# The activations' pool closed after the attention and opened again 64 bytes on

## The chip, the cores and the metric

The kernel runs on one core of a Trainium2 chip. The metric is the device time of one launch in microseconds (us). TensorE (PE) does matmuls, VectorE (DVE) and ScalarE (ACT) element-wise work, GpSimd (POOL) a little of it and DMA descriptors; SyncE (SP) only issues DMAs.

## The reference

Two layers over `x` of 512 tokens by 1024, all in fp32. The first is dilated attention, the second an mLSTM mixer; each is followed by a SwiGLU feed-forward block.

```python
def reference(x, ...):
    h = x
    h = h + dilated_attention_mixer(rms_norm(h, attn_norm[0]), positions, attn_w_in[0], attn_w_out[0])
    h = h + swiglu(rms_norm(h, ffn_norm[0]), ffn_w_in[0], ffn_w_out[0])
    h = h + mlstm_mixer(rms_norm(h, mlstm_norm[0]), mlstm_w_in[0], ..., mlstm_w_out[0])
    h = h + swiglu(rms_norm(h, ffn_norm[1]), ffn_w_in[1], ffn_w_out[1])
    return rms_norm(h, final_norm)

def swiglu(xn, w_in, w_out):           # D_FF = 2816
    gu = xn @ w_in
    return (jax.nn.silu(gu[..., :D_FF]) * gu[..., D_FF:]) @ w_out
```

## The kernel before, in words

**Arithmetic.** Each fp32 operand of a matmul is split in two fp32r parts, a high half (a copy on ACT, names in `_h`) and a low half (value minus high, on DVE, names in `_l`). A product is three matmuls: high by high, low by high, high by low (`SPLITS`). `h` is kept as eight tiles `h0` to `h7` of 128 features by 512 tokens. Normed activations `n1` (for the first feed-forward block) are split likewise into `n1_h0` to `n1_h3` and `n1_l0` to `n1_l3`, each holding two of the eight tiles; the norm's factor is applied after the product.

**Stages around the change.** The attention ends with the output projection: `awo0` to `awo3`, each 256 output features in two banks, from the split heads `ao_h0` to `ao_h3`, `ao_l0` to `ao_l3`. Its last part `awo3` runs through `project` (line 280): two chunks of four tiles, and for each chunk both banks. DVE adds each bank to `h` (line 1431), ACT squares `h` (`n1sq`, line 420), DVE sums the squares (`n1ssum`, line 421). Then `norm("ffn", 0, "n1", ssum)` (line 1981) takes eight tiles with `x_tiles` and splits `h` into them (lines 262 and 263), and `ffn_in` begins with `plain(0)`: the four banks `f0j0_00`, `f0j0_01`, `f0j0_10`, `f0j0_11` from `n1` and the split weights of `f0j0`, whose tiles have the same names with `_w`, `_h`, `_l` (in those the second digit is the chunk, and the first is gate or up). In the middle stands the sum over tokens for the norm (`n1ss`, then a Newton iteration from `n1v` to `n1dg` on DVE, then `n1bc` on PE).

**Order.** The scheduler of the framework sets the order of each engine's instructions: it takes what is ready by its own reckoning of releases, where the code doesn't tie instructions together (`fenced`, `run`, `issue_after`). Engines run their instructions strictly in that order and wait on semaphores.

**Places.** A pool takes its memory at the end of the one before it, and inside a pool a tag has a place, in the order in which tags are first used. The order of pools is `const`, `act`, `gap0` (64 bytes), `w`, `gap1` (448 bytes), `h`, `norm`, and after them the pools of the running stage (attention, `ffn0`, `mlstm`, `ffn1`). `act` has eight tags `x0` to `x7` of 4 KB a partition. They hold in turn `xa` and `ao` (attention), `n1`, the hidden tiles 3 to 10 of the first feed-forward block, `n2`, `yo`, `n3`, and hidden tiles again. The first user of the pool is `idle_w` with tag `x7` (line 108), so that `x7` lies at the pool's start and `x0` to `x6` behind it. A tile waits for the last reader of what lay in its place: `n1_h0` (tag `x0`) lies where `ao_h0` lay, and so on, pair by pair.

Of the kernel before, what the change touches and what calls it, by code (L numbers as in the profile page):

```python
# [11 lines left out]
F32 = mybir.dt.float32  # L12
# [5 lines left out]
P = 128  # L18
# [57 lines left out]
def tile_hybrid_dilated_attn_mlstm(  # L76
# [8 lines left out]
    def pool(stack, name, **kw):  # L85
        return stack.enter_context(tc.tile_pool(name=name, bufs=1, **kw))

    cp = pool(ctx, "const")
    xp = pool(ctx, "act")
    gap0 = pool(ctx, "gap0")  # L90
    wp = pool(ctx, "w")
    gap1 = pool(ctx, "gap1")
    ps = pool(ctx, "psum", space=bass.MemoryType.PSUM)


# [43 lines left out]
    def col(key, i):  # L139
        return cols[:, row_of[key] + i:row_of[key] + i + 1]  # L140
# [7 lines left out]
    def defer(n, fn):  # L148
        later.append((tick[0] + n, next(order), fn))
# [106 lines left out]
    def split_act(hi, lo, src, gain):  # L256

        if gain is None:
            nc.scalar.activation(hi, src, AF.Copy)
            nc.vector.tensor_tensor(lo, src, hi.bitcast(F32), op=ALU.subtract)  # L260
        else:
            nc.scalar.activation(hi, src, AF.Copy, scale=gain)
            nc.vector.scalar_tensor_tensor(lo, src, gain, hi.bitcast(F32), op0=ALU.mult, op1=ALU.subtract)

    def x_tiles(name):
        parts = [xp.tile([P, 2, SEQ], F32R, tag="x%d" % i, name="%s_%s%d" % (name, "hl"[i % 2], i // 2))
                 for i in range(KC)]
        return [[parts[k // 2 * 2 + part][:, k % 2] for k in range(KC)] for part in range(2)]
# [104 lines left out]
    def inverse_rms(v, name, box=None, then=None):  # L373

        r = npl.tile([P, TB], F32, tag="rtok", name=name + "r", bufs=2)
        rbc = npl.tile([P, SEQ], F32, tag="rbc", name=name + "rbc")
        parts = {}

        def finish():
            nc.vector.tensor_scalar(v, v, 1.0 / D, EPS, op0=ALU.mult, op1=ALU.add)  # L380
            rsqrt_newton(npl, v, TB, name + "r", r)
            rhl = npl.tile([P, 2, TB], F32R, tag="rhl", name=name + "rhl", bufs=2)
            nc.vector.tensor_copy(rhl[:, 0], r)
            nc.vector.tensor_tensor(rhl[:, 1], r, rhl[:, 0].bitcast(F32), op=ALU.subtract)
            for part in range(2):
                dg = parts[part] = npl.tile([P, SEQ], F32R, tag=("ssum", "sq")[part], name=name + "dg",
                                               bufs=1 + part)
                for tb in range(TB):
                    nc.vector.tensor_scalar(dg[:, tb * P:(tb + 1) * P], ident,
                                            rhl[:, part, tb:tb + 1].bitcast(F32), None, op0=ALU.mult)  # L390

        def hook():
            bp = ps.tile([P, 512], F32, tag="t", name=name + "bc", bufs=1)
            for part in range(2):
                nc.tensor.matmul(bp, ones_r, parts[part], start=(part == 0), stop=(part == 1))
            nc.vector.tensor_copy(rbc, bp)
            if then is not None:
                then(bp)
        if box is None:
            finish()  # L400
        else:
            box["finish"] = finish
        return rbc, r, hook


    w_in = attn_w_in[0]
    hp = pool(ctx, "h")
    npl = pool(ctx, "norm")
    h = [hp.tile([P, SEQ], F32, tag="h", name="h%d" % k, bufs=KC + 1) for k in range(KC)]

    def squares_of(name):

        ssum = npl.tile([P, SEQ], F32, tag="ssum", name=name + "ssum")

        def add(k):
            if k == 0:
                nc.scalar.activation(ssum, h[k], AF.Square)
            else:
                sq = npl.tile([P, SEQ], F32, tag="sq", name=name + "sq", bufs=2)
                nc.scalar.activation(sq, h[k], AF.Square)  # L420
                nc.vector.tensor_tensor(ssum, ssum, sq, op=ALU.add)
        return ssum, add
# [1057 lines left out]
    def norm(key, k0, name, ssum=None, wait=1):  # L1480
        pair = x_tiles(name)
        add = None
        if ssum is None:
            ssum, add = squares_of(name)
        for k in range(KC):
            split_act(pair[0][k], pair[1][k], h[k], col(key, k0 + k))
            if add is not None:
                add(k)
        v = npl.tile([P, TB], F32, tag="rs_v4", name=name + "v", bufs=2)
        box = {}  # L1490

        def sums():
            sp = ps.tile([P, 512], F32, tag="t", name=name + "ss", bufs=1)
            for tb in range(TB):
                nc.tensor.matmul(sp[:, tb:tb + 1], ssum[:, tb * P:(tb + 1) * P], ones[:, 0:1],
                                 start=True, stop=True)
            nc.vector.tensor_copy(v, sp[:, :TB])
            box["finish"]()
        rbc, r, hook = inverse_rms(v, name, box)
        defer(wait, sums)  # L1500
        return pair, rbc, r, hook
# [253 lines left out]
    def output_products(layer, fp, wo, sums_of_rows):  # L1755
# [222 lines left out]
            return [(kind, ops[(a, b) if kind == "product" else b], whl[a, b]) for kind, a, b in items[-TAIL:]]  # L1978
        return hid, during, prepare, work

    pair, rbc, _, hook = norm("ffn", 0, "n1", ssum)
    with ExitStack() as fctx:
        fp = pool(fctx, "ffn0")
# [25 lines left out]
        old, h = h, []  # L2009
# [565 lines left out]
```

## Time and profile before

| what | value |
|---|---|
| median of 3 runs | 1357.41 us (1357.39 to 1357.9) |
| the profiled execution's own time | 1358.57 us |
| its span | 1356.8 us |
| TensorE busy | 1340.1 us, 99% |
| VectorE busy | 1133.0 us, 84% |
| ScalarE busy | 813.3 us, 60% |
| GpSimd busy | 196.7 us, 14% |

The profile is of one execution. A row of a timeline has start and length in us, engine, line, operation, `out<-in` with buffer numbers left out (`n_h` is any of `n1_h0`, ...), shape and count, and in brackets the idle time before it with what ended it. A matmul's length is longer than the step to the next one, since matmuls are pipelined; the steps are read from starts, or from the chain of work that ended last, which has start, length and count of a run of matmuls.

### The profile page before, as it was taken

The numbers are of one execution on the slowest core, as the hardware profiler recorded it, in microseconds if no ns is written. First come the engines' busy times: TensorE is split into PE (matmuls) and PEld (weight loads), VectorE is DVE, ScalarE is ACT, GpSimd is POOL, SyncE is SP. The second block draws the span as 40 slices with busy tenths as digits, with TensorE's granted clock in tenths as the row PEclk, the third lists the DMA queues.
The fourth block names the chain that finished last, engine by engine and source line by source line (L and its number), as shares of the span: only waits on it lengthen the run. The fifth ranks groups of instructions, "written<-read, shape, count | busy, mean of one in ns | idle before, by whom it ended". The sixth has DMA issues, their size and how long they took to land.

```text
span 1356.8 us, 23343 instructions
## 1 busy us (share of the span) xinstructions
PE 1340.1 (99%) x9100; PEld 1222.1 (90%) x9100; DVE 1133.0 (84%) x1787; ACT 813.3 (60%) x1303; POOL 196.7 (14%) x272
## 2 busy tenths in 40 slices
PE   9999999999999999999999999999999999999997
PEld 7898899999988888999999998898878899999886
DVE  7988789899876389888888898898848988997887
ACT  6676577667674255555577464795534555558854
POOL 3000013141412001000010110122200112112113
PEclk9999999999999999999999999999999999999999
DMA  9354244554676357343362743324333545447863
GB/s 306 122 181 155 79 141 143 169 172 155 184 261 191 125 142 172 114 125 125 125 156 79 171 126 87 100 63 124 94 118 97 127 133 172 141 136 173 189 171 101
DMA packets 141270, 194.90 MB, mean 144 GB/s; under 512 B 9028, under 2 KB 106116, under 8 KB 141160
## 3 DMA queue, kind: packets, MB, share of 16 engines
q1 hardware_dynamic: 120128, 140.73, 33.0%
q0 software_dynamic: 19808, 52.48, 16.1%
q8 instruction: 71, 1.16, 0.3%
q10 hardware_dynamic: 1224, 0.21, 0.1%
q14 instruction: 39, 0.32, 0.1%
HBM read 167.30 MB, written 22.54 MB: 140 GB/s over the span
## 4 chain that ended last, share of the span: by engine, by line
PE 79%; DVE 10%; ACT 3%; issue 3%; DMA 1%; POOL 0%; SPq 0%; ACTq 0%; DVEq 0%; POOLq 0%
PE fo L1996 7%; PE f1j_u L1681 5%; PE f0j_u L1681 5%; PE f1j_c L1681 4%; PE f0j_c L1681 4%; PE f1j_p L1681 4%; PE f0j_p L1681 4%; PE mwo L275 3%; PE f1j L275 3%; PE f0j L275 3%; PE mqk L275 3%; PE awo L275 3%; PE finp L2411 3%; PE mo L275 3%; PE finc L2411 2%
## 5 line engine op out<-in xcount | busy, mean ns | idle before, releaser
L1803 POOL DMA_DIRECT2D f0S<-in_ffn_w_out_dram x10 | 8.7, 874 | 248.9 <-DVE f0hid L1720 162.3
L2364 POOL DMA_DIRECT2D hD<-hB x32 | 20.7, 655 | 109.6 <-DVE hB L2361 109.4
L1828 POOL DMA_DIRECT2D f1T<-in_ffn_w_out_dram x15 | 17.8, 1186 | 86.1 <-ACT f1T L1831 40.8
L240 DVE TENSOR_TENSOR v1P_l<-v1W,v1P_h 128x1024 fp32r<-128x1024 f32 x14 | 17.1, 1224 | 10.3 <-ACT v1P_h L238 10.3
L275 PE MATMUL mo<-n_h,mo_k_h 128*128 128x512 f32 x64 | 25.7, 401 | 0.0
L275 PE MATMUL mwo<-yo_h,mwo_k_h 128*128 128x512 f32 x64 | 25.5, 398 | 0.0
L275 PE MATMUL awo<-ao_h,awo_k_h 128*128 128x512 f32 x64 | 25.5, 398 | 0.0
L275 PE MATMUL mwo<-yo_l,mwo_k_h 128*128 128x512 f32 x64 | 25.5, 398 | 0.0
L275 PE MATMUL mwo<-yo_h,mwo_k_l 128*128 128x512 f32 x64 | 25.5, 398 | 0.0
L275 PE MATMUL mo<-n_h,mo_k_l 128*128 128x512 f32 x64 | 25.4, 397 | 0.0
L275 PE MATMUL mqk<-n_h,mqk_k_h 128*128 128x512 f32 x64 | 25.4, 397 | 0.0
L275 PE MATMUL mo<-n_l,mo_k_h 128*128 128x512 f32 x64 | 25.4, 396 | 0.0
L275 PE MATMUL mqk<-n_l,mqk_k_h 128*128 128x512 f32 x64 | 25.3, 396 | 0.0
L275 PE MATMUL awo<-ao_l,awo_k_h 128*128 128x512 f32 x64 | 25.3, 396 | 0.0
L275 PE MATMUL f0j<-n_h,f0j_h 128*128 128x512 f32 x64 | 25.3, 395 | 0.0
L275 PE MATMUL f1j<-n_h,f1j_h 128*128 128x512 f32 x64 | 25.3, 395 | 0.0
L275 PE MATMUL awo<-ao_h,awo_k_l 128*128 128x512 f32 x64 | 25.3, 395 | 0.0
L275 PE MATMUL mqk<-n_h,mqk_k_l 128*128 128x512 f32 x64 | 25.2, 394 | 0.0
L275 PE MATMUL f0j<-n_l,f0j_h 128*128 128x512 f32 x64 | 25.2, 394 | 0.0
L275 PE MATMUL f1j<-n_l,f1j_h 128*128 128x512 f32 x64 | 25.2, 394 | 0.0
L275 PE MATMUL f0j<-n_h,f0j_l 128*128 128x512 f32 x64 | 25.2, 394 | 0.0
L275 PE MATMUL f1j<-n_h,f1j_l 128*128 128x512 f32 x64 | 25.2, 394 | 0.0
(2746 smaller groups left out, 5999.6 us busy)
## 6 DMA issues: line engine op xcount, KB each, us to landing
f0j_w<-in_ffn_w_in_dram SPq DMA_DIRECT2D x17, 512.0 KB, 5.7
f1j_w<-in_ffn_w_in_dram SPq DMA_DIRECT2D x17, 512.0 KB, 6.9
f1T<-in_ffn_w_out_dram POOLq DMA_DIRECT2D x15, 512.0 KB, 6.4
f0hid<-in_ffn_w_in_dram SPq DMA_DIRECT2D x9, 512.0 KB, 6.1
f1hid<-in_ffn_w_in_dram SPq DMA_DIRECT2D x9, 512.0 KB, 5.0
v0W<-in_attn_w_in_dram SPq DMA_DIRECT2D x8, 512.0 KB, 6.8
v1W<-in_attn_w_in_dram SPq DMA_DIRECT2D x8, 512.0 KB, 3.7
awo_k_w<-in_attn_w_out_dram SPq DMA_DIRECT2D x8, 512.0 KB, 4.7
```

The costliest lines, as they stand in the source:

```text
L240: nc.vector.tensor_tensor(lo[:, :n], raw[:, :n], hi[:, :n].bitcast(F32), op=ALU.subtract)
L275: nc.tensor.matmul(acc, whl[a][:, k, m * P:(m + 1) * P], pairs[b][kk], start=(kk == 0 and (a, b) == SPLITS[0]), stop=(kk == nk - 1 and (a, ...
L1681: nc.tensor.matmul(acc[name][:, m * HALF:(m + 1) * HALF], whl[a][:, k, m * P:(m + 1) * P], ops[okey][b][:, k], start=(fresh and m == 0 and ...
L1803: nc.gpsimd.dma_start(t, src[1][:, ks], accum_op=ALU.add)
L1828: nc.gpsimd.dma_start(view(to), weight_rows(hk * UNITS + u, n), accum_op=ALU.add)
L1996: nc.tensor.matmul(acc, w[a_][:, k, m * P:(m + 1) * P], b[b_][k], start=(fresh and k == 0 and (a_, b_) == SPLITS[0]), stop=(k == 1 and (a_ ...
L2364: nc.gpsimd.dma_start(hD[k // 4].rearrange("(b i) x -> i b x", i=R)[:, :, c0:c0 + R], t[R * a_:R * (a_ + 1)])
L2411: nc.tensor.matmul(acc[m], a[a_][k][:, (2 * t + m) * P:(2 * t + m + 1) * P], w[b_][:, k, :], start=(fresh and k == 0 and (a_, b_) == SPLIT ...
```

## The change

The pool `act` moves behind `h` and `norm` and gets a stack of its own. When the attention has ended, it is closed and opened again as `act2`, with 64 bytes ahead of it and 64 bytes behind it (the two gaps are allocated and never used).

```diff
     cp = pool(ctx, "const")
-    xp = pool(ctx, "act")
     gap0 = pool(ctx, "gap0")
     wp = pool(ctx, "w")
     gap1 = pool(ctx, "gap1")
+    hp = pool(ctx, "h")
+    npl = pool(ctx, "norm")
+    xctx = ExitStack()
+    xp = pool(xctx, "act")
     ps = pool(ctx, "psum", space=bass.MemoryType.PSUM)
...
     w_in = attn_w_in[0]
-    hp = pool(ctx, "h")
-    npl = pool(ctx, "norm")
...
+    xctx.close()
+    gap3 = pool(ctx, "gap3")
+    gap3.tile([P, 16], F32, name="gap3")
+    xp = pool(ctx, "act2")
+    gap4 = pool(ctx, "gap4")
+    gap4.tile([P, 16], F32, name="gap4")
     pair, rbc, _, hook = norm("ffn", 0, "n1", ssum)
```

In bytes of a partition: `w`, `h` and `norm` come to lie 32768 lower, the attention's own pools stay, the pools of all later stages come to lie 128 higher. `act` goes from 18464 to 82720 for the attention and to 82784 after it. In the reopened pool the first tag used is `x0` (`n1_h0`) and `x7` comes last, so that `n1_h0` lies over the old `x7` (`ao_l3`) except for that one's first 64 bytes, and over the first 64 bytes of the old `x0`; each tile behind it lies likewise over two old ones, shifted.

No instruction is added or removed, and up to the end of the attention each engine's order is the same. It changes at one place, the join of `awo3` and `f0j0`. ScalarE there, before (`n1_h..<-h..` is a split of `h`, `f0j0_.._h` the high half of a weight):

```order
L420 ACTIVATE n1sq_4910<-h3_4751 128x512
L262 ACTIVATE n1_h0_4989<-h0_4745,cols_94 128x512
L420 ACTIVATE n1sq_4913<-h4_4753 128x512
L262 ACTIVATE n1_h0_4989<-h1_4747,cols_94 128x512
L262 ACTIVATE n1_h1_4991<-h2_4749,cols_94 128x512
L420 ACTIVATE n1sq_4916<-h5_4755 128x512
L262 ACTIVATE n1_h1_4991<-h3_4751,cols_94 128x512
L238 ACTIVATE f0j0_10_h_5032<-f0j0_10_w_5030 128x1024
L420 ACTIVATE n1sq_4983<-h6_4757 128x512
L262 ACTIVATE n1_h2_4993<-h4_4753,cols_94 128x512
L262 ACTIVATE n1_h2_4993<-h5_4755,cols_94 128x512
L238 ACTIVATE f0j0_01_h_5094<-f0j0_01_w_5092 128x1024
```

ScalarE at the same place now (its line 265 is line 262 of before, 241 is 238, 421 is 420):

```order
L421 ACTIVATE n1sq_4910<-h3_4751 128x512
L421 ACTIVATE n1sq_4913<-h4_4753 128x512
L241 ACTIVATE f0j0_10_h_5044<-f0j0_10_w_5042 128x1024
L421 ACTIVATE n1sq_4916<-h5_4755 128x512
L421 ACTIVATE n1sq_4983<-h6_4757 128x512
L241 ACTIVATE f0j0_01_h_5106<-f0j0_01_w_5104 128x1024
L265 ACTIVATE n1_h0_5001<-h0_4745,cols_100 128x512
L421 ACTIVATE n1sq_4986<-h7_4759 128x512
L265 ACTIVATE n1_h0_5001<-h1_4747,cols_100 128x512
L265 ACTIVATE n1_h1_5003<-h2_4749,cols_100 128x512
```

Before, six of the eight splits stand ahead of the high half of `f0j0_01`; now all eight stand behind it. `n1_h0` now waits for the last matmul of `awo3` (of `ao_h3` with the low half of the second chunk's weight), where it waited for the last one that reads `ao_h0`, thirty matmuls earlier; the high half of `f0j0_01` waits, before and now, for the last but one. VectorE at the same place now (a sum of `h` and a bank, low halves of weights and of `n1`):

```order
L422 TENSOR_TENSOR n1ssum_4902<-n1ssum_4902,n1sq_4983 128x512
L1432 TENSOR_TENSOR h7_4759<-awo3_1_4920,h7_4759 128x512
L243 TENSOR_TENSOR f0j0_01_l_5107<-f0j0_01_w_5104,f0j0_01_h_5106 128x1024
L266 SCALAR_TENSOR_TENSOR n1_l0_5002<-h0_4745,cols_100,n1_h0_5001 128x512
L422 TENSOR_TENSOR n1ssum_4902<-n1ssum_4902,n1sq_4986 128x512
L266 SCALAR_TENSOR_TENSOR n1_l0_5002<-h1_4747,cols_100,n1_h0_5001 128x512
L266 SCALAR_TENSOR_TENSOR n1_l1_5004<-h2_4749,cols_100,n1_h1_5003 128x512
L266 SCALAR_TENSOR_TENSOR n1_l1_5004<-h3_4751,cols_100,n1_h1_5003 128x512
```

Before, the low halves of `f0j0_10` and `f0j0_01` came after all eight of `n1`; now they come ahead of them, and no low half of `n1` stands ahead of `h7`. TensorE at the join now:

```order
L278 MATMUL awo3_1_4920<-ao_h3_4640,awo3_k1_l_4954 128x512
L278 MATMUL f0j0_00_5037<-n1_h0_5001,f0j0_00_h_5033 128x512
L278 MATMUL f0j0_01_5038<-n1_h0_5001,f0j0_00_h_5033 128x512
L278 MATMUL f0j0_10_5039<-n1_h0_5001,f0j0_10_h_5044 128x512
L278 MATMUL f0j0_11_5040<-n1_h0_5001,f0j0_10_h_5044 128x512
L278 MATMUL f0j0_00_5037<-n1_l0_5002,f0j0_00_h_5033 128x512
L278 MATMUL f0j0_00_5037<-n1_h0_5001,f0j0_00_l_5034 128x512
L278 MATMUL f0j0_00_5037<-n1_h0_5001,f0j0_00_h_5033 128x512
L278 MATMUL f0j0_01_5038<-n1_l0_5002,f0j0_00_h_5033 128x512
```

Before, the twelve matmuls of `f0j0_00`'s first chunk came first and then the twelve of `f0j0_01`; now the first matmul of each of the four banks comes first, and the next ones alternate between `f0j0_00` and `f0j0_01`.

## The prediction

> **What bounds the kernel now.** I read the page's head first, then the list of waits of TensorE, then the chain that ended last around the place of the change, then the timelines of three engines there. On the page, the span, the busy row and the granted clock (tenths, in forty slices):
>
> ```profile
> span 1356.8 us, 23343 instructions
> PE 1340.1 (99%) x9100; PEld 1222.1 (90%) x9100; DVE 1133.0 (84%) x1787; ACT 813.3 (60%) x1303; POOL 196.7 (14%) x272
> ...
> PEclk9999999999999999999999999999999999999999
> ```
>
> TensorE (PE) is busy in 99% of the span. The list of waits, first over the whole span and then from 478 us on, says what is left of idle time:
>
> ```profile
> PE a1s L792 <- POOL a1g_k L642: 1.4, 1, 1.4
> ...
> PE fo L1996 <- ACT fo L2019: 0.3, 1, 0.3
> PE m6yT L371 <- DVE m6yt L2285: 0.2, 1, 0.2
> ```
>
> The last two rows are all that PE waits for between 478 us and the end: 0.5 us. So from the attention's end on nothing stands between matmuls, a stall put in there moves everything behind it, and at most 0.5 us of it can be given back later. The chain (start, length, what) shows the join of the two stages:
>
> ```profile
> 458.23 22.41 PE awo L275 x96
> 480.64 5.60 PE f0j L275 x24
> 486.24 0.78 PE n1ss L1495 x8
> 487.02 8.50 PE f0j L275 x36
> 495.52 0.46 PE n1bc L395 x2
> ```
>
> Here the first feed-forward matmul follows the last output projection without a gap; 96 matmuls in 22.41 us is 0.2334 us each. It can do that because ScalarE (ACT) and VectorE (DVE) split `h` into `n1` while `awo` still runs:
>
> ```profile
> 473.68 0.73 ACT L262 ACTIVATE n_h<-h,cols 128x512 fp32r<-128x512 f32 x1 [1.41 <-PE awo L275]
> ...
> 478.66 0.63 ACT L420 ACTIVATE n1sq<-h 128x512 f32<-128x512 f32 x1 [0.42 <-DVE h L1431]
> 479.27 1.34 ACT L262 ACTIVATE n_h<-h,cols 128x512 fp32r<-128x512 f32 x2
> 480.52 1.04 ACT L238 ACTIVATE f0j_h<-f0j_w 128x1024 fp32r<-128x1024 f32 x1
> 481.47 0.63 ACT L420 ACTIVATE n1sq<-h 128x512 f32<-128x512 f32 x1
> 482.00 1.32 ACT L262 ACTIVATE n_h<-h,cols 128x512 fp32r<-128x512 f32 x2
> ```
>
> The first `n1` split starts at 473.68, 7 us ahead of its use. It was released by `awo`: thirty matmuls of 0.2334 (7.0 us) before the last one, when the first of the `ao` tiles had been read for the last time.
>
> **The change, part by part.** *Places alone* (the tiles of the w, h and norm pools lie 32 KB lower, those of the feed-forward pools 128 bytes higher, the act tiles elsewhere): no instruction is added or removed on any engine. I cost it at nothing, and bound it below.
>
> *The wait.* In the old pool the place of `x7` comes first, since `idle_w` took it first; then `x0` to `x6`. In the reopened pool `n1_h0` (`x0`) comes first, 64 bytes on. So it lies over the old `x7`, which is `ao_l3`, and `ao_l3` is read to the end of the attention. The order rows say the same: on ACT no `n1` split stands ahead of the split of `f0j0_01` any more, and all eight come behind it. Their new release is the last `awo` matmul, which the chain ends at 480.64.
>
> *ACT.* The split of `f0j0_01` waits for the last but one `awo` matmul (its buffer held `awo3_k1_h`), so it starts at 480.64 - 0.23 + 0.04 = 480.45; 0.04 us is what ACT needed after the release at 473.68 (473.64 by counting back thirty matmuls). It holds ACT for 481.47 - 480.52 = 0.95, so the first `n1_h0` starts at 481.40 and ends at 482.13, by 0.73. In the old program PE was at 480.48 then (its row below). The square of `h7` (0.53) and the other seven halves (0.61 each, since two in a row show 1.32 and one 0.71) follow; the second is done at 481.40 + 0.61 + 0.53 + 0.71 = 483.25.
>
> *DVE.* The rows for its durations and steps:
>
> ```profile
> 480.68 0.69 DVE L1431 TENSOR_TENSOR h<-awo,h 128x512 f32<-128x512 f32 x1 [0.18 <-PE awo L275]
> 481.28 1.41 DVE L263 SCALAR_TENSOR_TENSOR n_l<-h,cols,n_h 128x512 fp32r<-128x512 f32 x2
> 482.61 0.69 DVE L421 TENSOR_TENSOR n1ssum<-n1ssum,n1sq 128x512 f32<-128x512 f32 x1
> 483.21 1.41 DVE L263 SCALAR_TENSOR_TENSOR n_l<-h,cols,n_h 128x512 fp32r<-128x512 f32 x2
> 484.53 2.35 DVE L240 TENSOR_TENSOR f0j_l<-f0j_w,f0j_h 128x1024 fp32r<-128x1024 f32 x2
> 487.06 0.16 DVE L1497 COPY n1v<-n1ss 128x4 f32<-128x4 f32 x1 [0.17 <-PE n1ss L1495]
> ...
> 490.94 1.65 DVE L389 TENSOR_SCALAR n1dg<-cst,n1rhl 128x128 fp32r<-128x128 f32 x8
> ```
>
> A low half of `n1` takes 0.75 and steps by 0.67, a weight's low half steps by 1.14 (2.35 for two, 1.22 for one), a sum by 0.60. In the new order the low half of `f0j0_01` stands ahead of the first `n1_l0`. It starts when ACT is done with the high half, at 480.45 + 1.04 + 0.03 = 481.52; so `n1_l0` starts at 482.66 and is there at 483.41, its second half (a sum between) at 484.68, then one each 0.67.
>
> *PE.* Its rows at the join, one matmul each:
>
> ```profile
> 480.25 0.39 PE L275 MATMUL awo<-ao_h,awo_k_l 128*128 128x512 f32 x1
> 480.48 0.40 PE L275 MATMUL f0j<-n_h,f0j_h 128*128 128x512 f32 x1
> 480.71 0.39 PE L275 MATMUL f0j<-n_l,f0j_h 128*128 128x512 f32 x1
> ```
>
> In the new order four matmuls that need only `n1_h0` come first: one for each of `f0j0_00`, `01`, `10`, `11`. The first starts at 482.17 instead of 480.48: 1.69 us of stall. The fifth needs `n1_l0`, there at 483.41; PE would be ready at 482.17 + 4 x 0.2334 = 483.10, and starts at 483.44. The fifth would have run at 480.48 + 0.93 = 481.41, so PE is now 2.03 us behind. The next low half is due at 484.71 for a matmul that PE reaches at 484.84, the next at 485.38 for 485.54: it just holds, by 0.13 to 0.2. I add 0.07 us for a restart after a wait and take **+2.1 us**. Below it lies +0.9, should ACT take `n1_h0` at 480.68 before the weight (then 0.73 for the half); above it +3.3, should two more DVE steps of 0.60 stand in the way of the low halves.
>
> *What is late next.* The sums for the norm (`n1ss`) come two matmuls later in PE's order and 2.1 us later in time; DVE's chain from `n1v` at 487.06 to the end of `n1dg` at 492.59 is 5.53 us long with one weight's low half in it, as before. From 489.6 it ends at 495.1, and `n1bc` comes up on PE at about 497.3: 2.2 us to spare, before 495.52 - 492.59 = 2.9. The weight load for `j2` on SP is issued earlier, since the low half of `f0j0_10` now comes earlier on DVE; SP and POOL keep their order. Nothing else waits, so the 2.1 us stay.
>
> *Places, bounded.* In these rows the operands lie in different pools, and so differently against 64, 128 and 512 bytes: `f0hl` and `f0w_hl` both in the feed-forward pool, `mv_k` and `n_h` in w and act, and on DVE `f0hid` and `f0j_w` across pools against `f0j_w`, `f0j_h` in one:
>
> ```profile
> 804.28 0.40 PE L1996 MATMUL fo<-f0hh,f0w_hl 128*128 128x512 f32 x1
> 804.51 0.40 PE L1996 MATMUL fo<-f0hl,f0w_hl 128*128 128x512 f32 x1
> ...
> 805.67 0.40 PE L360 MATMUL mv<-mv_k_h,n_h 128*128 128x512 f32 x1
> 805.91 0.40 PE L360 MATMUL mv<-mv_k_l,n_h 128*128 128x512 f32 x1
> ...
> L1652 DVE TENSOR_TENSOR f0j_w<-f0hid,f0j_w 128x1024 f32<-128x1024 f32 x9 | 11.0, 1221 | 0.1
> L240 DVE TENSOR_TENSOR f0j_l<-f0j_w,f0j_h 128x1024 fp32r<-128x1024 f32 x8 | 9.7, 1221 | 1.2 <-ACT f0j_h L238 1.2
> ```
>
> 0.23 and 0.24 us from one start to the next, 1221 and 1221 ns: no place is seen to cost anything. But some stages do keep another step (chain again, count at the end):
>
> ```profile
> 862.37 5.66 PE mv L329 x48
> ...
> 1024.32 5.60 PE f1j L275 x24
> ...
> 1133.05 2.72 PE f1j_u L1681 x24
> ...
> 1272.06 2.75 PE finp L2411 x12
> ```
>
> These are 118 ns and 113 ns for 256 columns, 233 and 229 ns for 512, and I can't say from what. That gives the ends: 960 matmuls of line 275 (`f0j`, `f1j`, `mqk`, `mo`, `mwo`, 192 each) read an operand in act; at 229 they would save 4.0 us, with 192 of line 329 at 113 another 0.9. The same size the other way costs 4.0. Zero is nearest to the rows, and I take it. The Trainium skill, "SBUF — State Buffer", section "Who interferes with whom", has TensorE with two read ports of its own and says that "PE and ACT never wait on anyone". By that rule the places are worth nothing and the sum stays at +2.1; the equal rows above agree, the 229 against 233 neither way.
>
> **The rivals.**
>
> *The places speed up the matmuls.* For it: the steps of 229 and 113 ns above exist in this very trace. Against it: equal steps over unequal places. Worth -4.9 + 2.1 = -2.8, so 1354.6; with the 3024 matmuls of line 1681 drawn in too, more.
>
> *The places slow them down*, ending on the other side. Place: line 275's stages, where act and w come to lie alike against 128 bytes. Price: +4.0 + 2.1, so 1363.5. It decides as soon as their step is 0.7 ns longer (960 x 0.7 = 0.67 us, with 2.1 over the bound of 2.7).
>
> *The pause lowers TensorE's clock.* The program's start shows what that costs:
>
> ```profile
> 1.51 4.63 PE L114 MATMUL idle<-idle_w,ones_r 128*128 128x512 f32 x10 [1.51 <-DVE idle_w L109]
> ```
>
> Ten matmuls in 4.63 us are 0.46 us each, 0.23 more than later; ten such after the pause would add 2.3, so 1361.8. Against it: no slice of the clock row above falls below 9, with waits of 1.4 us at `a1s` and 1.51 here; but it shows 9 for this slow stretch too, so it says little. The Trainium skill, "TensorE: Matmul & The Clock Gate", Part 1, halves the clock after an idle window of about 3.4 us; by that rule a pause of 1.7 us keeps it, and the sum stays.
>
> *The change adds no stall*: 1357.4. Only if a part of `n1` were split before 480.64, and the order shows none.
>
> **How the numbers follow.** The profiled execution took 1358.57 us, its span 1356.8; that is 1.16 above the median of 1357.41 of the runs. The sum, made against its rows, gives 1360.7 for it, and 1357.4 + 2.1 = 1359.5 for the median. Changes within 0.2% (2.7 us) are about what a measurement of this kernel can't tell from none. Chances: the stall alone 0.65, and of it 0.11 over +2.7 and the rest, 0.54, within; no stall 0.04; places faster 0.14, of which 0.12 beyond -2.7; places slower 0.12; the clock 0.05. So faster 0.12, within 0.60, slower 0.28. The range of 8 in 10 leaves out most of both place cases: 1356.0 to 1362.0; the likeliest case alone has 1358.3 to 1360.7.
>
> **What would show it.** In the changed kernel's list of waits PE has a new row for `f0j` on ACT's `n1_h`, of 1.5 to 2, and a small one on DVE's `n1_l`. The first `f0j` starts 1.7 us behind the end of `awo`. The chain names ACT and DVE for about 2 us there. Every later stage stands 2.1 us later, with steps of 233 and 113 ns as before. It is wrong if those steps move, if the pause is over 3 us, or if `n1bc` becomes a wait.

## The result and the profile after

The changed kernel took 1372.0 us (median of 5 runs, 1370.62 to 1372.9) against 1357.89 of the kernel before on the same chip (5 runs): a ratio of 1.0105, interval 1.009 to 1.0119. It is 1.05% slower; I had forecast 1359.5 with a range up to 1362.0.

The head of the page of the changed kernel's profile:

```profile
span 1368.8 us, 23344 instructions
...
PE 1351.5 (99%) x9100; PEld 1237.6 (90%) x9100; DVE 1133.7 (83%) x1787; ACT 813.8 (59%) x1303; POOL 196.9 (14%) x272
...
PEclk9999999999999999999999999999999999999999
```

The span is 12.0 us longer than in the profile before, TensorE is busy 11.4 us longer with the same 9100 matmuls, and the other engines within 1 us of where they were. So most of the time went into TensorE's steps and not into its waits. (The two profiled executions took 1358.57 and 1370.62 us; the second is the shortest of its five, so the medians lie 14.1 us apart. What follows accounts for the 12.) Of TensorE's waits of more than 0.5 us one is new (us in total, times, longest):

```profile
PE f0j L278 <- ACT n_h L265: 1.5, 1, 1.5
```

At the join of the two stages (timeline of PE):

```profile
479.62 1.21 PE L278 MATMUL f0j<-n_h,f0j_h 128*128 128x512 f32 x4 [1.52 <-ACT n_h L265]
480.93 0.50 PE L278 MATMUL f0j<-n_l,f0j_h 128*128 128x512 f32 x1
481.27 0.40 PE L278 MATMUL f0j<-n_h,f0j_l 128*128 128x512 f32 x1
481.51 0.39 PE L278 MATMUL f0j<-n_h,f0j_h 128*128 128x512 f32 x1
```

That is the stall. The last `awo` matmul starts at 477.70 here, so the first `f0j` starts 1.92 us behind it where it was 0.23 (the 1.52 in the brackets is counted from that matmul's end): 1.69 us. The fifth matmul comes 1.31 behind the first instead of 0.93, and the sixth 0.34 behind it instead of 0.23: 2.2 us in all. The rest of the new time is in the chain that ended last:

```profile
912.64 5.74 PE mv L332 x48
...
1035.16 8.28 PE f1j L278 x36
...
1073.85 2.83 PE f1j_c L1682 x24
1076.68 2.83 PE f1j_p L1682 x24
...
1265.99 2.80 PE finp L2418 x12
```

Here `f1j` takes 230 ns in this row where it took 233 (226.8 over the whole stage, from starts), line 1682 (line 1681 of before) takes 118 where it took 113, and `finp` 233 where it took 229. The table has the same from the starts of all matmuls, summed over each line (lines of before). Its rows come to 12.4 us; with -0.3 from all other lines that makes the 12.1 us by which the first and the last matmul start further apart.

| line, stage | matmuls | step before, ns | step after, ns | change, us |
|---|---|---|---|---|
| 1681, hidden products | 3024 | 113.3 | 117.8 | +13.5 |
| 2411, last outputs | 420 | 228.9 | 233.3 | +1.9 |
| 1996, first outputs | 888 | 114.0 (256 columns) | 116.2 | +1.2 |
| 275, from act, with the stall of 2.2 | 1200 | 233.3 | 227.3 (where act was reopened) | -3.1 |
| 1343, values | 336 | 233.3 | 228.9 | -1.3 |
| 329, 360 | 480 | 117.6; 229.2 | 119.6; 227.1 and 229.2 | +0.2 |

In the text below "distance" is the place of a matmul's moving operand less that of its stationary one, in steps of 32 bytes, modulo 16 steps (512 bytes). The operands of a stage share it, since all tiles are multiples of 512 bytes apart. The change moved line 1681 from 6 to 10, line 275 from 14 to 8 after the attention, line 2411 from 10 to 6.

### The profile page after: what moved, and what is told of

The parts are those of the page before. It is cut to its first block, busy times and chain, and to the rows that moved or that the text cites. A ratio compares the mean times of both kernels' runs of the same rounds, so it can differ in the third digit from the quotient of the medians.

```text
span 1368.8 us, 23344 instructions
## 1 busy us (share of the span) xinstructions
PE 1351.5 (99%) x9100; PEld 1237.6 (90%) x9100; DVE 1133.7 (83%) x1787; ACT 813.8 (59%) x1303; POOL 196.9 (14%) x272
```

## The experiments

Three theories. **A**: the distance alone sets the step. **C**: the 32 KB by which `w` was moved, or traffic of other engines, does it. **B**, formed when the first four runs had refuted A and the 32 KB (other engines' traffic was left to the map of matmuls below): TensorE's stream has two steady patterns, 113.3 and 117.8 ns for 256 columns, and the way in which a run of matmuls begins decides which one it holds. For the stall: it comes from the tile that `n1_h0` lies over (my reason), or from the pool being given back as a whole.

### The stall's reason: x7 taken first

```diff
     xp = pool(ctx, "act2")
+    xp.tile([P, 2, SEQ], F32R, tag="x%d" % (KC - 1), name="first")
```

> The changed kernel, but in the reopened pool the place of x7 is taken first, so that n1_h0 lies over the old x0 and x1 (ao_h0, ao_l0), which are read for the last time some thirty matmuls before the attention's end, and no longer over ao_l3. My prediction's reason for the stall (n1_h0 lies over ao_l3): TensorE's wait of 1.5 us for f0j on ACT's n_h is gone and the time falls by about 2 us, to 1370. Rival (a pool that is given back is waited for as a whole, so it doesn't matter which old tile lies below): the wait of 1.5 us stays and the time stays at 1372. Either way line 1681's step stays at 118 ns.

Measured: 1372.85 us (4 runs), ratio to before 1.012 (1.0103 to 1.0136). The timeline of PE:

```profile
480.28 1.19 PE L278 MATMUL f0j<-n_h,f0j_h 128*128 128x512 f32 x4 [1.53 <-ACT n_h L265]
481.59 0.66 PE L278 MATMUL f0j<-n_l,f0j_h 128*128 128x512 f32 x1
482.05 0.63 PE L278 MATMUL f0j<-n_h,f0j_l 128*128 128x512 f32 x1
482.48 0.63 PE L278 MATMUL f0j<-n_h,f0j_h 128*128 128x512 f32 x1
```

The wait is still there, 1.53 us, although `n1_h0` now lies over tiles that are read for the last time long before. So my reason was wrong: which old tile lies below makes no difference. What is left is the rival, that the old pool is waited for as a whole. It is inferred: the trace shows only that ScalarE splits the weight of `f0j0_01` first and goes on to `n1_h0` without idle time, in an order that was set beforehand. A further run below, with nearly the same places and the pool not given back, has no such wait.

A second thing stands in these rows: behind the pause seven matmuls step by 0.43 us, where they stepped by 0.23 in the changed kernel behind the same pause. A finer view of the granted clock (third number from the end; in front of it the engines' busy times) shows why:

```profile
482.00:484.00 2.00, 2.00 (x6) 1.56 (x5) 2.00 (x4) 2.00 (x4) 0.00 (x0) 0.50 0.86 258
```

TensorE's clock was halved there, and 24 matmuls on this kernel is 1.6 us behind the changed one, counted from the last `awo`. The row of the page, with slices of 34 us, shows 9 throughout. In the profile of the changed kernel the same view has 1.00 from 476 to 486 us.

### 128 bytes alone

```diff
+    gap3 = pool(ctx, "gap3")
+    gap3.tile([P, 32], F32, name="gap3")
     pair, rbc, _, hook = norm("ffn", 0, "n1", ssum)
```

> The kernel before with nothing but an unused 128 bytes ahead of the feed-forward pools: act, w, h and norm stay where they were, nothing is given back. Distance theory (a matmul's step is set by how far its moving and its stationary operand lie apart modulo 256 or 512 bytes): line 1681 goes from 113.3 to 117.8 ns (3024 matmuls, +13.5 us), the final projections of line 2411 from 228.9 to 233.3 (420, +1.9), line 1996 from 114 to 116 (836, +1.8), line 275 stays at 233.2; in all +17 us, 1375. Rival (the 32 KB by which the w pool was moved does it): no step moves, 1358.

Measured: ten runs from 1357.5 to 1373.9, median 1360.6, ratio 1.0048 (1.002 to 1.0076). The runs lie in groups: 1357.5 to 1357.9, 1360.1 to 1360.8, 1364.8 to 1366.4, 1372.5 to 1373.9. The profiled one (1360.1) has, at distance 10,

```profile
525.30 2.72 PE f0j_c L1681 x24
528.02 2.72 PE f0j_p L1681 x24
```

113.3 ns. Theory A falls with this: the same distance as in the changed kernel, and the other step. Line 2411 went to 233.3 as expected. Line 1343, untouched and ahead of the edit, ran at 228.9 in this profile and at 233.3 in that of the kernel before, with the same addresses.

### 32 KB alone

```diff
-    xp = pool(ctx, "act")
...
     npl = pool(ctx, "norm")
+    xp = pool(ctx, "act")
```

> Only the order of the pools: act is opened behind h and norm and kept to the end, with no gap. So w, h and norm lie 32 KB lower as in the changed kernel, act lies at another place, but its distance to w changes from 14 to 6 steps of 32 bytes (modulo 16), and the feed-forward pools lie where they did. Distance theory: line 1681 stays at 113.3, line 275 at 233.2, line 2411 at 228.9; only line 1343 goes from 233.3 to 229 as in the changed kernel (336 matmuls, -1.4 us); about 1356.5. Rival (the 32 KB of w does it): line 1681 at 117.8, +13.5 us, about 1371.

Measured: 1357.19 us (10 runs), ratio 1.0003 (0.9993 to 1.0012), line 1681 at 113.3, line 275 at 233.3. The 32 KB alone do nothing to line 1681.

### Another 64 and 192 bytes

To the edit before this one, `gap2` of 64 bytes ahead of `act` and `gap3` of 192 behind it.

> As the run with act behind norm and kept open, with 64 unused bytes ahead of act and 192 behind it: act then lies against w as in the changed kernel's later stages, in all stages, the attention's output projection too, and the later pools lie 256 bytes further instead of 128. Distance theory modulo 256 bytes: line 275 at 227.5 instead of 233.2 (1150 matmuls, -6.6 us), line 1681 stays at 113.3, line 2411 at 229, line 1343 at 229 (-1.4), line 329 at 119.6 instead of 117.6 (+0.4); nothing waits at the join: about 1350, faster than both kernels. Rival (the 32 KB of w does it): 1365 or more. If the distance counts modulo 512, not 256, line 1681 moves to something else than 113.3 (3 us for each ns).

Measured: 1361.22 us (6 runs, 1359.7 to 1368.9), ratio 1.0049 (1.0027 to 1.0072); the forecast of 1350 failed. Line 275 did get faster (226.8 in `f0j` and `f1j`). Of line 1681 the first layer ran at 117.8 throughout, and in the second the chain shows the step change in the middle of a stage, with nothing about the places changing:

```profile
1075.41 2.83 PE f1j_p L1685 x24
1078.23 2.81 PE f1j_u L1685 x24
1081.04 2.72 PE f1j_c L1685 x24
1083.76 2.72 PE f1j_u L1685 x24
```

The change comes at a start that is 181 ns behind the one before it instead of 118, a wait of some 60 ns; from there to the stage's end it stays at 113.3. Theory B comes from these rows.

### Matmuls alone

Two kernels without any of the reference's work: only blocks of matmuls.

> A kernel that computes nothing of the reference: only blocks of matmuls of ones in the kernel's pattern (three products of two parts, twelve to an output half), 48 of 256 columns or 36 of 512, with nothing else running. In blocks named q (256 columns) and h (512) the moving operand starts 0 to 15 times 32 bytes (letters a to p) past a multiple of 512 bytes from the stationary one; each block waits for a VectorE copy of the one before, three rounds x, y, z. In blocks named t, 36 of 512 columns at one distance run straight into 48 of 256 at another; in blocks named u, one matmul of 16 to 128 columns stands between 512 columns at distance 8 and 256 at 10. Theory A (the distance alone sets the step): each letter has one step in all three rounds, 113.3 at g and o, 117.8 at c and k, about 119.6 at i, and for 512 columns 233.3 at g and o, 229 at c and k, 227 at i. Theory B (two steady patterns, and the start of a run of matmuls decides which one it falls into, for as long as nothing interrupts it): the same letter shows 113.3 in one round and 117.8 in another, and in t blocks the second part depends on the first. Rival C (ACT's, VectorE's and the DMAs' traffic makes the difference): with nothing else running all letters have one step.

The chain of it, blocks by name (start, length, count):

```profile
98.51 5.72 PE qgx L111 x48
...
339.83 5.93 PE qgy L111 x48
...
746.72 14.13 PE tagx L111 x84
...
862.14 14.12 PE tggx L111 x84
...
876.51 14.33 PE tgkx L111 x84
...
1439.95 14.02 PE ub L111 x85
...
1454.22 14.23 PE uc L111 x85
```

`qgx` and `qgy` are the same 48 matmuls at the same distance 6: 113.3 ns in the first round, 117.8 in the other two (steps from starts; the lengths differ by 47 x 4.45 ns = 0.21 us). With nothing else running, that leaves theory B of the three. `tggx` and `tgkx` differ by 0.21 us = 47 x 4.45 ns: out of 512 columns at 233.3 the 256-column part ran at 113.3 at distance 6 and at 117.8 at 10. Out of 512 columns at 226.7 (`tagx`) or 228.9 it ran at 117.8 at each distance tried (2, 6, 10, 14). And in `ub`, a single matmul of 32 columns in between brought distance 10 to 113.3; one of 48 (`uc`) did not (16 and 96 columns did, 64 and 128 did not). The steps of the q and h blocks repeat every 8 letters, 256 bytes, but for places that show two values (mean step from starts, the first six of a block and the first block of all left out):

| distance modulo 8 | 256 columns, ns | 512 columns, ns |
|---|---|---|
| 0 | 119.9 | 226.7 |
| 1 | 116.7 | 233.3 |
| 2 | 117.8 | 228.9 |
| 3 | 120.0 | 233.3 |
| 4 | 118.8 or 120.0 | 233.3 or 232.6 |
| 5 | 117.3 or 118.7 | 234.5 |
| 6 | 113.3 or 117.8 | 233.3 |
| 7 | 118.3 | 233.3 |

> Again only blocks of matmuls of ones, nothing of the reference. Each block: 24 matmuls of 512 columns (names vx: at distance 8, which ran at 226.7; vy: at 6, which ran at 233.3), then without a pause 24 of 256 columns at distance 6, 10 or 14 (third letter g, k, o), one short matmul of 8, 16, 24, 32, 40, 48, 56, 64, 80, 96, 112 or 128 columns (fourth letter a to l), 36 of 256 columns, the same short one again, 36 more. Theory B (two steady patterns, and what moves TensorE's phase chooses): the first part runs at 117.8 in vx blocks and at 113.3 in vy blocks at distance 6, as in the map before; behind the short one the step is 113.3 for some column numbers and 117.8 for others, whatever the distance to the pattern's start, and stays so until the next short one. Rival (the pattern is set once by the stage ahead): no short matmul changes it.

Measured, in steps worked out from starts: at distances 6 and 14 a short matmul of 64, 80 or 96 columns took 113.3 to 117.8 in 12 cases of 12, and 117.8 to 113.3 in 9 of 12; 112 columns left either as it was in 8 of 8. For the shortest, 8 to 56 columns, it hung on what came before: behind the stage at 226.7 the first short one changed nothing and the second did. Out of the stage at 233.3, 12 of 24 blocks at distances 6 and 14 began at 113.3, where I had expected all of those at 6. At distance 10 no short one at that same distance freed it from 117.8. The rival (the pattern is set once by the stage ahead) falls.

### The places back in the kernel

To the edit of "32 KB alone": 64 bytes ahead of `act` and 448 behind it; then 64 and 64; then 0 and 128.

> The kernel with act behind norm, kept open, 64 unused bytes ahead of it and 448 behind it: act lies against w as in the changed kernel's later stages (distance 8, line 275 at 226.7 ns), and the later pools lie 512 bytes further, so that line 1681 has distance 6 again as in the kernel before. Theory A (distance alone): line 1681 at 113.3, time 1350. Theory B (the pattern is taken over from the stage ahead, which runs at 226.7): line 1681 at 117.8 in one or both of its stages of 1512 matmuls, 6.7 us each, so 1357 or 1363 and not the same in each run.

Measured: 1367.79 us (6 runs, two of them 1359.3 and 1361.1, four 1367.1 to 1369.2), ratio 1.0076 (1.0059 to 1.0093). Line 1681 is back at the old kernel's distance 6, and yet the first layer runs at 117.8 throughout, and the second begins so. Modulo 512 bytes this kernel differs from that of "32 KB alone" by the 64 bytes ahead of `act` and by nothing else, and the order of instructions is the same. The chain where the second layer's stage begins, first with the 32 KB alone and then here:

```profile
1069.10 2.73 PE f1j_c L1681 x24
...
1072.67 2.83 PE f1j_c L1685 x24
```

So it is the place of `act`, which line 275 reads ahead of the stage, that decides how line 1681 begins here. (In this execution, of 1361.1 us, the small wait in the second layer then brought it to 113.3.)

> The changed kernel's places without giving the pool back: act is opened once, 64 bytes behind norm, and 64 more bytes lie behind it, so n1 and the feed-forward pools lie exactly where they do in the changed kernel's later stages, in the order of instructions of the kernel before, with no wait at the join. If the places with the stage ahead make the slow step, line 1681 stays at 117.8 and the time is about 1371 less the stall of 1.9 and less about 1.1 for the attention's own 192 projections: 1368. If the stall itself (a pause that shifts TensorE's pattern) makes it, line 1681 is back at 113.3: about 1354.

Measured: 1369.13 us (4 runs), ratio 1.0083 (1.0068 to 1.0098), line 1681 at 117.8 in both layers, and no wait of `f0j` at the join. The stall isn't what starts the slow pattern.

> As the run before in this list, but with act without the 64 bytes ahead of it and all 128 behind it: line 275 keeps distance 6 and its 233.3 ns, line 1681 has the changed kernel's distance 10. Theory A (distance alone): line 1681 at 117.8, 1371. Theory B (taken over from the stage ahead, which runs at 233.3): 113.3 in most runs, 1357 to 1360, as the run with the 128 bytes alone.

Measured: 1367.02 us (4 runs), ratio 1.0068 (1.0053 to 1.0083); I had expected 1357 to 1360. The chain:

```profile
526.84 2.72 PE f0j_c L1683 x24
...
1039.62 30.80 PE f1j L279 x132
1070.41 2.82 PE f1j_c L1683 x24
1073.24 2.83 PE f1j_p L1683 x24
```

Both layers come out of 132 matmuls at 233.3, at the same distance 10; the first ran at 113.3, the second at 117.8. So "taken over from the stage ahead" is too simple at distance 10: either pattern can come out there.

### One short matmul in the real kernel

In the changed kernel, ahead of the first matmul of line 1682's stage in each layer (the bank is started anew behind it):

```diff
+                if name == "c11" and fresh and j == PLAIN:
+                    nc.tensor.matmul(acc[name][:, :32], whl[0][:, 0, 0:P], pair[0][0][:, :32], start=True, stop=False, ...)
```

> The changed kernel with one matmul more ahead of each of the two stages of line 1681 (one per feed-forward layer): 32 columns of n1 or n3 at distance 8, into a bank that the next matmul starts anew. In the map a short one of 32 columns there brought distance 10 to 113.3 ns, where without it it ran at 117.8. Theory B: the first layer's 1512 matmuls run at 113.3, 6.7 us less; the second layer's start so too, and whether they stay there past the small wait (about 60 ns) behind their first 48 is open: 1365 or 1358.6 in all. Theory A (places alone) and the rival that the 32 KB of w do it: no change, 1372.

Measured: 1371.08 us (6 runs, two of them 1361.5 and 1363.4), ratio 1.0079 (1.0054 to 1.0105). The chain of the second layer, in one of the long executions:

```profile
1076.57 0.02 PE f1j_c L1680
1076.59 2.82 PE f1j_c L1685 x24
1079.41 2.72 PE f1j_p L1685 x24
1082.13 2.84 PE f1j_u L1685 x24
1084.97 2.83 PE f1j_c L1685 x24
```

Behind the short one (one step of 201 ns, which the first row includes) the step is 113.3, as in the map, and some 50 matmuls on it is 117.8 again; in the first layer it held for about 95, until waits (starts 222 to 421 ns apart). So the short matmul does choose the pattern; small waits in the stage then choose again.

The strongest test is the kernel before, with every place as it was:

```diff
+                if name == "p5" and fresh and j == PLAIN:
+                    nc.tensor.matmul(acc[name][:, :96], whl[0][:, 0, 0:P], ops[okey][0][:, 0][:, :96], start=True, stop=False, ...)
```

> The kernel before, every place as it was, with one matmul of 96 columns more ahead of the second product of line 1681 in both layers (into a bank that the next matmul starts anew). In the map 96 columns brought 113.3 ns to 117.8 at distance 6 in the blocks that started at 117.8 and were at 113.3 by a first short one. Theory B: both layers' stages go to 117.8 from their 24th matmul on and stay: 1488 x 4.45 ns = 6.6 us each, 1370 in all, as slow as the changed kernel. Theory A (the places set the step): 1357.

Measured: 1373.88 us (5 runs, 1372.4 to 1374.5), ratio 1.0119 (1.01 to 1.0138). The chain:

```profile
525.92 2.73 PE f0j_c L1684 x24
528.66 0.04 PE f0j_p L1679
528.70 2.90 PE f0j_p L1684 x24
531.60 2.83 PE f0j_u L1684 x24
...
1292.26 2.80 PE finp L2414 x12
```

Two matmuls of 96 columns, some 0.08 us of work together, make the kernel 17 us slower: 2976 x 4.45 ns = 13.2 of it in line 1681, from the short one to the end of each layer's stage. Even `finp`, at its old distance 10, now takes 233 instead of 229 (line 2411: +1.9), and line 1996 (256 columns) 116.2 instead of 114.0 (+1.4). So the slow step needs none of the changed places.

### A faster version?

The places of the run with 64 and 448 bytes, where line 275 is fast, with a short matmul of 96 columns in each layer; then the second layer's one a pair later; then both there.

> The run with 64 bytes ahead of act and 448 behind it (line 1681 at distance 6, entered at 117.8 from the stage at 226.7), with one matmul of 96 columns more ahead of the second product of line 1681 in both layers, on the product's own operands. In the map 96 columns brought 117.8 to 113.3 at distance 6, and 113.3 to 117.8. Theory B: the first layer's stage goes to 113.3 from its 24th matmul on (-6.6 us); the second's goes there too, until the small wait behind its 48th matmul puts it on one or the other pattern: 1361 or 1354, by runs. Theory A: no change from 1368.

Measured: 1359.61 us (12 runs: three at 1351.1 to 1352.4, nine at 1358.1 to 1361.3), ratio 1.0006 (0.999 to 1.0023).

> The same, but in the second layer the short matmul comes one hidden pair later, behind the small wait. In the run without it about four of six executions were slow in both layers (1367 to 1369) and two in one alone (1359 to 1361). Theory B: the first layer at 113.3; the second is swapped, so that the executions that the wait had left at 117.8 go to 113.3 and the others the other way: most at 1354, some at 1360. If it beats the kernel before (1357) in the median, it is the fastest here.

Measured: 1360.43 us (12 runs: two at 1352.7 and 1353.3, seven at 1359.4 to 1360.9, three at 1367.5 to 1369.0), ratio 1.0027 (1.0006 to 1.0048). The profiled one took 1353.3, and its chain shows the second layer being freed:

```profile
1081.22 2.83 PE f1j_u L1688 x24
1084.04 2.83 PE f1j_c L1688 x24
1086.87 0.04 PE f1j_p L1683
1086.91 2.81 PE f1j_p L1688 x24
1089.73 2.72 PE f1j_u L1688 x24
```

> The run with one short matmul ahead of the second product in both layers, and in the second layer a further one a hidden pair later, behind the small wait. Without the further one 9 of 12 executions took 1358 to 1361, with the second layer's stage at 117.8 in the one profiled, and 3 took 1351 to 1352. Theory B: the further one swaps the pattern, so about 9 of 12 take 1352 and 3 take 1360; the median is 1352, faster than both kernels. Rival (the second layer's pattern doesn't hang on the phase there): median 1360 as without it.

Measured: 1360.58 us (12 runs: eight at 1359.5 to 1361.0, four at 1367.7 to 1368.9), ratio 1.0045 (1.0026 to 1.0064). Not one came to 1352. The profiled one was at 113.3 behind the small wait, and the further short matmul put it at 117.8:

```profile
1083.34 2.72 PE f1j_c L1688 x24
1086.06 0.04 PE f1j_p L1683
1086.10 2.89 PE f1j_p L1688 x24
1089.00 2.83 PE f1j_u L1688 x24
```

So the swap works both ways, but which pattern the small wait leaves isn't the same from kernel to kernel nor from execution to execution. A version that is reliably faster than the kernel before was not found; the fastest executions (1351.1) show that 5 to 6 us are there.

## Why the prediction was wrong, point by point

- **Bounded by TensorE, no slack behind the attention**: held. The new time is TensorE's own, and nothing gave it back.
- **The stall**: the size was right (2.1 forecast, 2.2 in the profile: 1.69 before the first `f0j` as forecast, and 0.5 behind it where I had 0.34 + 0.07), and so was the course on ScalarE, the weight's split first and then `n1_h0`; no `n1bc` wait came. The reason that I gave was wrong. I put it on `ao_l3` under `n1_h0`; with other tiles under it the wait was 1.53. Giving the pool back makes the wait: with `act` kept open it is not there. That the whole pool is waited for is the reading that is left.
- **Places, "Zero is nearest to the rows, and I take it"**: this is the step that failed. It was worth +10 us net: +13.5 in line 1681, +1.9 and +1.2 in two output stages, about -5 in line 275, -1.3 in line 1343 (this last is not the places' work: with its old places the line ran at 228.9 too, as in the kernel before with two short matmuls). What the runs showed in place of zero: the 64 bytes brought line 275 to its fastest step, and the stage behind it then began, and stayed, in the slower of its two patterns. The equal rows that I weighed, 0.23 and 0.24 us, were two points of a map with two steps for one place; the 1221 ns are VectorE's and say nothing of TensorE. The rows that told of it stood beside them, 118 against 113 and 233 against 229; I said that I couldn't say from what, and still priced them only through line 275. With 3024 matmuls line 1681 was the largest stage that the change moved, and 3024 x 4.45 = 13.5 us was to be worked out as a loss as well.
- **The rival "places slow them down"** had the right sign and the wrong place: I tied it to line 275, which became faster (233.3 to 227.3, -6.0 ns; the 229 of the faster rival was nearly right), while the loss was in line 1681, which only the faster rival named.
- **The clock rival**: the changed kernel's profile shows no slow step behind its pause of 1.52 us, and a granted clock of 1.00. One other profile does, behind 1.53: seven steps of 0.43 instead of 0.23, with the clock at 0.50, 1.6 us where I had priced 2.3. I had reckoned that a pause of 1.7 us keeps the clock; in that execution a shorter one did not. It is at most a term of that size. Whether the changed kernel's other four executions, 0.9 to 2.3 us longer than the profiled one, had it isn't known.
- **The rule of the Trainium skill, "SBUF — State Buffer", section "Who interferes with whom"**, that TensorE waits for no other engine, is not contradicted: the two patterns appear with nothing else running. What I drew from it, that places are worth nothing, was wrong: the step hangs on the distance between the two operands of TensorE's own matmuls (226.7 to 234.5 ns at 512 columns in the map).

As far as the runs show, the stage ahead decides how line 1681 begins. In the profiles, out of 512 columns at 226.8 ns line 1681 began at 117.8 in all 16 stages in which no short matmul stood ahead of it (both layers of the changed kernel and of seven others). Out of 233.3 ns it began at 113.3 in nine of ten (both layers of the kernel before, with and without the short matmuls, of the 128 bytes alone and of the 32 KB alone, and one layer of the run with 0 and 128 bytes). The change took line 275 from the second case to the first. In the map, too, 117.8 was all that followed 226.7, and 233.3 was followed by either.

What the runs leave open: what in TensorE or its memory reads makes the two patterns; and why 233.3 isn't always followed by the same one. Of executions without a profile only the time is known: 1355.4 to 1360.1 for the kernel before, with one at 1364.2, and 1370.6 to 1372.9 for the changed one. In the map no short matmul at distance 10 itself brought that distance from 117.8 to 113.3. A kernel whose places shut out the slower pattern was not found and, beyond the runs above, not tried.

## What to carry to other kernels

When a trace shows two steps for matmuls of one size, 4% apart, price the difference over the largest such stage before taking "places" for nothing: here 4.45 ns x 3024 outweighed all the rest. A change of some bytes, one short matmul or a wait of 60 ns can swap the pattern of a whole stage, as it did here, so a difference of 1% between two versions of a TensorE-bound kernel may say little about what the edit was meant to do; look at the steps in both traces, and at the spread over runs in groups, before crediting or blaming it. And the pool that was given back here made its next tenant late, wherever in it the new tile lay; reckon with the last reader of the whole pool.

## What the runs showed of the hardware

- One and the same run of matmuls of 256 columns steps by 113.3 or by 117.8 ns, and keeps either for over a thousand matmuls; at 512 columns 228.9 and 233.3 were both seen at distance 10 (line 2411 in the kernel before, without and with the two short matmuls). Both differences are 4.45 ns a matmul, 13.3 ns for the three matmuls of one product.
- The step hangs on the distance of the moving and the stationary operand modulo 256 bytes: 226.7 to 234.5 ns at 512 columns, 113.3 to 120.0 at 256. The distance that is fastest at 512 columns (0) is among the slowest at 256.
- A matmul of 64 to 96 columns, some 0.04 us, swapped the pattern at distances 6 and 14 in 21 cases of 24; one of 112 in none of 8.
- An idle time of TensorE of 1.53 us was followed in one execution by a granted clock of 0.50, for about 3.4 us (the stretch of the steps of 0.43 us); an idle time of 1.52 us in another was not.
